# Whole-row spectrum stores, a later lambda product and bias loads on another queue in a two-block transformer kernel

## The chip, the cores and the metric

The kernel runs on one core of a Trainium2 chip. The core has a matrix engine (PE, with a separate track PEld for loading weights), a vector engine (DVE), an activation engine (ACT), a general engine (POOL) and a synchronising engine (SP). SP, ACT and POOL also issue DMA transfers; the trace calls these queues SPq, ACTq and POOLq. Each engine runs its own instructions strictly in order. The metric is device time in microseconds for one execution, and lower is better.

## The reference, cut to what matters

Two transformer blocks run over 512 tokens of 1024 features. The first has four mixers (a differential attention, a neighbourhood attention, a pooling and a long convolution), then a mixture of experts; the second has windowed attention and a state-space branch. The change touches the first block's opening: the filters of the long convolution, the modulation vectors, and one scalar of the differential attention.

```python
def hyena_filters(L, w1, b1, w2, b2, w3, b3):
    ...
    h = jnp.sin(HY_SIN_FREQ * (z @ w1.astype(F32) + b1.astype(F32)))
    h = jnp.sin(HY_SIN_FREQ * (h @ w2.astype(F32) + b2.astype(F32)))
    h = (h @ w3.astype(F32) + b3.astype(F32)).reshape(L, HY_ORDER, 2, HY_CH)
    ...
def bidir_long_conv(u, h_fwd, h_bwd, d_skip):
    k = jnp.concatenate([h_fwd, jnp.zeros_like(h_fwd[:1]), h_bwd[:0:-1]], axis=0)
    y = jnp.fft.irfft(jnp.fft.rfft(uf, n=2 * L, axis=1) * jnp.fft.rfft(k, axis=0)[None], ...)[:, :L]
...
mod_l = jnp.split(jax.nn.silu(c) @ lp['ada_w'] + lp['ada_b'], 6, axis=-1)
lam = jnp.exp(jnp.sum(lv[0] * lv[1])) - jnp.exp(jnp.sum(lv[2] * lv[3])) + lam_init
```

The filters go through two small layers with a sine, and a third layer. Their spectrum (real and imaginary part, for two convolutions) is wanted later, when the convolution multiplies in the frequency domain. `mod_l` scales and shifts the normed tokens, so that no projection can start before it.

## The kernel before, in words

The stage concerned is the opening, roughly the first 100 of 1294 us. The order of each engine's instructions is written by a planner that follows the program's order as a priority and fills in later instructions when it believes an engine free; so an instruction can run ahead of lines that stand above it (DVE runs L851 to L852 before L471). `tc.issue_after(x)` puts the instructions of its block behind `x` on x's engine.

- **Loads.** SP issues the small filter weights, the decay table, four blocks of x (L441), two of ctx (L444), eight blocks of `ada_w` of 1 MB each (L448), then the later weights. ACT issues `vec`, `ident`, `misc`, `rowsb` (L243, a row broadcast to 128 partitions) and the four loads of the modulation bias into `ab0` (L454). POOL issues the Fourier tables.
- **Filter layers** (L465 to L480): for each layer PE multiplies, ACT adds the bias (L469), five DVE instructions reduce the angle (L471 to L475), and ACT takes the sine. The DVE folding of the third layer's weights (L487) is held behind the last of these by `hold`.
- **Lambda product** (L851, recorded at the helper's line L252): DVE multiplies two parts of `rowsb`, and L852 sums them; the exponential comes much later (L854).
- **Third layer and filters** (L493 to L502), then `fold_filter` (a fold by DVE, a cast by ACT and a remainder by DVE, through the helper `split`, L254 to L256), for part 1 (sine) and part 0 (cosine) of convolutions o = 0 and 1.
- **Spectra** (`spectrum`, L574): for each part, o and half f2, PE forms two blocks of 128 frequencies by 256 channels, ACT copies them into a tile `ko` (two buffers, L581), and an ACT-issued DMA stores `ko` into the DRAM buffer `kspec` (256 KB). For part 0, f2 = 0, an extra row, the top frequency, is stored at frequency row 0 in the columns of part 1 (L588). Before the change the part 1, f2 = 0 store leaves that row out, with two DMAs: partitions 1 to 127, and row 0's second block.
- **Modulation**: PE multiplies the eight `ada_w` blocks between the spectra (L346); DVE adds the bias `ab0` (in `ada_end`, recorded at L249, tile `ab`); PE transposes (L363), and `norm_k` transposes and scales the tokens (L528 to L535). Then the projections begin.

Of the kernel before, what the change touches and what calls it, by code (L numbers as in the profile page):

```python
# [224 lines left out]
def tile_model(ctx: ExitStack, tc: tile.TileContext, A, out):  # L225
    nc = tc.nc
    V, SC, G, SY, TE = nc.vector, nc.scalar, nc.gpsimd, nc.sync, nc.tensor
# [23 lines left out]
    def mul(o, a, b, eng=None):  # L251
        (eng or V).tensor_tensor(o, a, b, op=ALU.mult)  # L252
# [79 lines left out]
    def nm(s="t"):  # L332
        bn[0] += 1
        return f"{s}{bn[0]}"
# [50 lines left out]
    def dft_mm(ps, tbl, part, fc, vh, vl, dfx, mid=None):  # L385
        fs = slice(fc * P, fc * P + P)
        sg = int(part != (fc >= 2))
        x = (None, (0, 1), (1, 0), (1, 0))[fc] if part == 0 else (None, None, (2, 1), (2, 1))[fc]
        for tt in (1, 0):
            mm3(ps, tbl[:, 0, tt, fs], tbl[:, 1, tt, fs], vh[:, sg, tt], vl[:, sg, tt], tt == 1,  # L390
                tt == 0 and x is None)
            if tt == 1 and mid is not None:
                mid()
        if x is not None:
            c = dfx[0:1, x[0] * P:x[0] * P + P]
            TE.matmul(ps, c, vh[0:1, x[1], 0], start=False, stop=False)
            TE.matmul(ps, c, vl[0:1, x[1], 0], start=False, stop=True)

    def nyq_mm(ps, altc, vh, vl, alone):
        for n, (tt, v) in enumerate(((0, vh), (0, vl), (1, vh), (1, vl))):  # L400
            TE.matmul(ps, altc, v[:, 0, tt], start=alone and n == 0, stop=alone and n == 3)
# [8 lines left out]
    with tc.tile_pool(name="pz", bufs=8, space=PSUM, reuse_waits="tile") as pz, \  # L410
            tc.tile_pool(name="fl", bufs=1, side="right", reuse_waits="tile") as fl, \
            tc.tile_pool(name="nrm", bufs=1, reuse_waits="tile") as nrm:
        def bank0():
            return pz.tile([P, 512], F32, tag="b", name=nm("pz"))
# [36 lines left out]
        ab0 = fl.tile([P, S], F32, name="ab0")  # L451
        G.memset(ab0, 0.0)
        for j in range(4):
            SC.dma_start(ab0[32 * j:32 * j + 2], A["ada_b"][0:1, 512 * j:512 * j + 512]  # L454
                         .partition_broadcast(2).rearrange("p o f -> p (o f)"))
        dfx = fl.tile([1, 384], F32R, name="dfx")
        G.dma_start(dfx, A["dfx"][:, 0:384])
# [7 lines left out]
        for layer, w in ((0, fw1), (1, fw2)):  # L465
# [9 lines left out]
            hold = V.tensor_scalar(f, f, PI_SAFE, -PI_SAFE, op0=ALU.min, op1=ALU.max)  # L475
# [8 lines left out]
        with tc.issue_after(hold.ins):  # L484
            for n, op in ((0, ALU.add), (1, ALU.subtract)):
                f3 = fw3.rearrange("p (o d c) -> p o d c", o=2, d=2)
                V.tensor_tensor(w3[:, :, n], f3[:, :, 0], f3[:, :, 1], op=op)  # L487
        fw3 = w3.rearrange("p o d c -> p (o d c)")


        filt = fl.tile([P, 4, 2, 2, 256], F32, name="filt")
# [82 lines left out]
        def spectrum(n, part, o, f2):  # L574
            ph, pl = phs[n]
            c0 = o * 512 + part * 256
            ko = fl.tile([P, 2, 256], F32, tag="ko", name=nm("ko"), bufs=2)
            for j in range(2):
                ps = bank0()[:, :256]
                dft_mm(ps, tbls[part], part, 2 * f2 + j, ph, pl, dfx)  # L580
                SC.copy(ko[:, j], ps)  # L581
            dst = kspec[2 * f2:2 * f2 + 2, :, c0:c0 + 256].rearrange("f p c -> p f c")
            if f2 == 0 and part == 0:
                V.tensor_scalar_mul(ko[0:1, 0], ko[0:1, 0], 0.5)
                ps = bank0()[0:2, :256]
                nyq_mm(ps, altc, ph, pl, True)
                V.tensor_scalar_mul(row0[:, o], ps[0:1], 0.5)
                SC.dma_start(kspec[0, 0:1, c0 + 256:c0 + 512], row0[:, o])  # L588
            if f2 == 0 and part == 1:
                SC.dma_start(dst[1:], ko[1:])  # L590
                SC.dma_start(dst[0:1, 1], ko[0:1, 1])
            else:
                SC.dma_start(dst, ko)

        steps = ((1, 0), (1, 1), (0, 0), (0, 1))
        aps = bank0()
# [2 lines left out]
        for f2 in range(2):  # L599
            spectrum(0, *steps[0], f2)  # L600
            ada_mm(f2, aps, araw[f2])
        filt_norms()
        for f2 in range(2):
            spectrum(1, *steps[1], f2)
            ada_mm(2 + f2, aps, araw[2 + f2])
# [11 lines left out]
        for k in range(4):  # L617
            spectrum(2 + k // 2, *steps[2 + k // 2], k % 2)
            norm_k(2 + k)
# [228 lines left out]
    lam = root.tile([P, 4], F32, name="lam")  # L848
    lp = root.tile([P, 2, 32], F32, name="lp")
    lv = rowsb[:, 16:144].rearrange("p (a b d) -> p a b d", a=2, b=2)  # L850
    mul(lp, lv[:, :, 0], lv[:, :, 1])  # L851
    V.tensor_reduce(lam[:, 0:2], lp, axis=AX.X, op=ALU.add)  # L852
    with tc.issue_after(hold_l.ins):
        SC.activation(lam[:, 0:2], lam[:, 0:2], AF.Exp)  # L854
# [1436 lines left out]
```

## Time and profile before

| what | us |
|---|---|
| median of 3 runs | 1297.05 |
| lowest and highest run | 1296.15, 1300.52 |
| the profiled execution, its own time | 1295.71 |
| its span in the profile | 1293.8 |

The profiled execution's time is 1.91 us more than its span, which lies around the profiled instructions. The granted PE clock was 0.946 of full speed over the span. Times in the trace count from the start of the span.

### The profile page before, as it was taken

The numbers are of one execution on the slowest core, as the hardware profiler recorded it, in microseconds if no ns is written. First come the engines' busy times: TensorE is split into PE (matmuls) and PEld (weight loads), VectorE is DVE, ScalarE is ACT, GpSimd is POOL, SyncE is SP. The second block draws the span as 40 slices with busy tenths as digits, with TensorE's granted clock in tenths as the row PEclk, the third lists the DMA queues.
The fourth block names the chain that finished last, engine by engine and source line by source line (L and its number), as shares of the span: only waits on it lengthen the run. The fifth ranks groups of instructions, "written<-read, shape, count | busy, mean of one in ns | idle before, by whom it ended". The sixth has DMA issues, their size and how long they took to land. (4 is left out here: it accounts for less than half of the span.)

```text
span 1293.8 us, 16003 instructions
## 1 busy us (share of the span) xinstructions
PE 1118.5 (86%) x5904; PEld 807.1 (62%) x5904; DVE 837.2 (65%) x1498; ACT 514.7 (40%) x907; POOL 210.4 (16%) x204
## 2 busy tenths in 40 slices
PE   3859979998588893999998999589799888899997
PEld 1447966675367772557464675368567676777785
DVE  3654365655678667428475897566954987977754
ACT  4252244443364232315243462344457332443532
POOL 1223500001610023100000000041400343130100
PEclk9978989999699996999999999899899999889999
DMA  9532714536612383988989995455121222223421
GB/s 345 199 106 81 174 62 135 195 131 193 180 50 98 99 272 117 314 305 325 367 305 384 334 353 205 156 196 173 50 65 46 82 78 82 78 78 119 153 70 65
DMA packets 132721, 220.61 MB, mean 171 GB/s; under 512 B 23645, under 2 KB 64793, under 8 KB 128795
## 3 DMA queue, kind: packets, MB, share of 16 engines
q1 hardware_dynamic: 122789, 196.04, 44.2%
q0 software_dynamic: 7104, 21.00, 5.5%
q10 hardware_dynamic: 2742, 2.46, 0.6%
q8 instruction: 49, 0.80, 0.3%
q14 instruction: 37, 0.30, 0.1%
HBM read 205.26 MB, written 11.04 MB: 167 GB/s over the span
## 5 line engine op out<-in xcount | busy, mean ns | idle before, releaser
L246 DVE TENSOR_TENSOR wl<-raw,wh 128x1024 fp32r<-128x1024 f32 x94 | 117.7, 1258 | 92.0 <-ACT wh L255 86.6
L255 ACT CAST wh<-raw 128x1024 fp32r<-128x1024 f32 x94 | 97.1, 1047 | 141.3 <-PE pf L260 66.0
L259 PE MATMUL pf<-r,wh 128*128 128x512 f32 x304 | 127.3, 421 | 8.1 <-DVE sg L252 3.0
L260 PE MATMUL pf<-r,wh 128*128 128x512 f32 x304 | 125.6, 414 | 0.7 <-DVE r L246 0.6
L261 PE MATMUL pf<-r,wl 128*128 128x512 f32 x304 | 125.4, 413 | 0.0
L249 DVE TENSOR_TENSOR r<-r,pb 128x512 f32<-128x512 f32 x88 | 55.0, 681 | 38.0 <-PE pb L1594 37.9
L259 PEld LDWEIGHTS pf<-r,wh 128*128 128x128 f32 x304 | 60.1, 198 | 24.9 <-DVE sg L252 3.5
L259 PE MATMUL pb<-wh,gh 128*128 128x512 f32 x176 | 70.5, 401 | 1.4 <-ACT wh L255 1.3
L260 PE MATMUL pb<-wl,gh 128*128 128x512 f32 x176 | 70.0, 398 | 0.8 <-DVE wl L246 0.7
L261 PE MATMUL pb<-wh,gl 128*128 128x512 f32 x176 | 69.9, 397 | 0.1
L260 PEld LDWEIGHTS pf<-r,wh 128*128 128x128 f32 x304 | 60.5, 199 | 15.1 <-DVE r L246 1.7
L261 PEld LDWEIGHTS pf<-r,wl 128*128 128x128 f32 x304 | 60.0, 197 | 14.7 <-issue 1.3
L246 DVE TENSOR_TENSOR wl<-r,wh 128x1024 fp32r<-128x1024 f32 x36 | 42.8, 1218 | 12.2 <-ACT wh L255 12.0
L255 ACT CAST wh<-r 128x1024 fp32r<-128x1024 f32 x36 | 37.1, 1054 | 22.4 <-DMA r<-in_moe_w_dram 12.8
L259 PE MATMUL ps<-r,wh 128*128 128x512 f32 (+1 forms) x112 | 44.0, 393 | 1.6 <-ACT at L867 1.5
L867 ACT COPY at<-ps 128x512 f32<-128x512 f32 x64 | 28.4, 481 | 40.4 <-PE ps L866 40.2
L261 PE MATMUL ps<-r,wl 128*128 128x512 f32 (+1 forms) x112 | 42.7, 381 | 0.0
L260 PE MATMUL ps<-r,wh 128*128 128x512 f32 (+1 forms) x112 | 42.6, 381 | 0.0
L259 PEld LDWEIGHTS pb<-wh,gh 128*128 128x128 f32 x176 | 33.2, 189 | 10.4 <-ACT wh L255 1.9
L1244 PE MATMUL pb<-xr,gw 128*64 128x512 f32 x136 | 39.6, 627 | 0.0
L1244 PE MATMUL pb<-r,gw 128*64 128x512 f32 x136 | 38.1, 598 | 1.3 <-DMA r<-in_moe_w_dram 1.3
L260 PEld LDWEIGHTS pb<-wl,gh 128*128 128x128 f32 x176 | 33.2, 189 | 9.3 <-DVE wl L246 1.9
(687 smaller groups left out, 2833.4 us busy)
## 6 DMA issues: line engine op xcount, KB each, us to landing
r<-in_moe_w_dram SPq DMA_DIRECT2D x42, 1024.0 KB
xr<-in_moe_w_dram SPq DMA_DIRECT2D x36, 1024.0 KB
raw<-in_w_in_dram SPq DMA_DIRECT2D x27, 1024.0 KB
r<-in_ada_w_dram SPq DMA_DIRECT2D x22, 1024.0 KB
raw<-in_moe_w_dram SPq DMA_DIRECT2D x18, 1024.0 KB
raw<-in_w_out_dram SPq DMA_DIRECT2D x8, 1024.0 KB
tb<-in_dft_dram POOLq DMA_DIRECT2D x4, 1024.0 KB, 7.1
itb<-in_idft_dram POOLq DMA_DIRECT2D x2, 1032.0 KB, 9.0
```

The source lines that it names most:

```text
L246: (eng or V).tensor_tensor(o, a, b, op=ALU.subtract)
L249: return (eng or V).tensor_tensor(o, a, b, op=ALU.add)
L255: SC.copy(hi, src)
L259: TE.matmul(ps, lh, rh, start=start, stop=False)
L260: TE.matmul(ps, lh, rl, start=False, stop=False)
L261: TE.matmul(ps, ll, rh, start=False, stop=stop)
L867: SC.copy(at[:, a:a + n].rearrange("p k q -> p (k q)"), pt[:, :n * P])
L1244: TE.matmul(ps[c], lh[:, k, c], raw[:, k * 512:k * 512 + 512], start=first and k == 0, stop=last and k == 3)
```

## The change

Three edits. The bias loads into `ab0` are issued by SP instead of ACT. The lambda product is held behind the last DVE instruction of the second filter layer. The part 1, f2 = 0 spectra are stored as whole tiles in one DMA each, so that row 0 of part 1 is first stored with that tile's row and later written over by the top-frequency row.

```diff
         for j in range(4):
-            SC.dma_start(ab0[32 * j:32 * j + 2], A["ada_b"][0:1, 512 * j:512 * j + 512]
+            SY.dma_start(ab0[32 * j:32 * j + 2], A["ada_b"][0:1, 512 * j:512 * j + 512]
                          .partition_broadcast(2).rearrange("p o f -> p (o f)"))
...
         fw3 = w3.rearrange("p o d c -> p (o d c)")
+        hold_f = hold
...
                 SC.dma_start(kspec[0, 0:1, c0 + 256:c0 + 512], row0[:, o])
-            if f2 == 0 and part == 1:
-                SC.dma_start(dst[1:], ko[1:])
-                SC.dma_start(dst[0:1, 1], ko[0:1, 1])
-            else:
-                SC.dma_start(dst, ko)
+            SC.dma_start(dst, ko)
...
     lv = rowsb[:, 16:144].rearrange("p (a b d) -> p a b d", a=2, b=2)
-    mul(lp, lv[:, :, 0], lv[:, :, 1])
+    with tc.issue_after(hold_f.ins):
+        mul(lp, lv[:, :, 0], lv[:, :, 1])
     V.tensor_reduce(lam[:, 0:2], lp, axis=AX.X, op=ALU.add)
```

## Rows read from the trace of the kernel before

**Rows 1.** The page: the span, and PE's busy time, share and instructions

```profile
span 1293.8 us, 16003 instructions
PE 1118.5 (86%) x5904; PEld 807.1 (62%) x5904; DVE 837.2 (65%) x1498; ACT 514.7 (40%) x907; POOL 210.4 (16%) x204
```

**Rows 2.** Stretches: length, busy per engine (instructions), granted PE clock, DMA share, GB/s

```profile
21.98:37.40 15.42, 13.99 (x17) 5.70 (x18) 8.23 (x14) 12.64 (x22) 4.88 (x4) 1.00 1.01 424
37.40:49.00 11.60, 11.60 (x69) 5.62 (x69) 10.13 (x17) 2.55 (x5) 6.36 (x3) 1.00 0.91 325
49.00:51.10 2.10, 2.10 (x15) 1.70 (x15) 2.10 (x9) 1.51 (x4) 0.00 (x0) 1.00 0.01 4
51.10:58.70 7.60, 7.60 (x59) 5.07 (x62) 2.31 (x9) 0.03 (x1) 0.00 (x0) 1.00 0.06 19
120.00:160.00 40.00, 40.00 (x275) 35.86 (x274) 17.41 (x25) 9.14 (x14) 18.93 (x39) 1.00 0.64 151
600.00:800.00 200.00, 193.13 (x859) 121.89 (x858) 145.63 (x187) 83.63 (x105) 3.95 (x4) 1.00 0.86 317
```

**Rows 3.** Timeline of PE after 56 us (start, length, work, [idle before and releaser])

```profile
56.54 2.78 PE L346 MATMUL pz<-r,sc 128*32 128x512 f32 x24
75.49 1.08 PE L363 MATMUL pz<-ident,ab 128*128 128x128 f32 x4 [16.17 <-ACT ph L255]
76.37 1.06 PE L528 MATMUL pz<-ident,xs 128*128 128x128 f32 x4
...
88.12 0.60 PE L528 MATMUL pz<-ident,xs 128*128 128x128 f32 x4
```

**Rows 4.** Timeline of DVE around the modulation bias

```profile
74.10 0.69 DVE L246 TENSOR_TENSOR ph<-fold,ph 128x512 fp32r<-128x512 f32 x1 [12.42 <-ACT ph L255]
74.71 0.68 DVE L249 TENSOR_TENSOR ab<-ab,pz 128x512 f32<-128x512 f32 x1
```

**Rows 5.** Timeline of ACT and its queue, 50 to 75 us

```profile
51.05 7.64 ACTq L591 DMA_DIRECT2D kspec<-ko  x1
58.73 0.37 ACT L581 COPY ko<-pz 128x256 f32<-128x256 f32 x1 [7.60 <-issue]
...
59.15 0.40 ACTq L593 DMA_DIRECT2D kspec<-ko  x1
59.59 0.61 ACT L255 CAST ph<-fold 128x512 fp32r<-128x512 f32 x1
64.23 0.65 ACT L581 COPY ko<-pz 128x256 f32<-128x256 f32 x2 [4.03 <-DMA kspec<-ko]
...
65.18 7.62 ACTq L591 DMA_DIRECT2D kspec<-ko  x1
72.90 0.65 ACT L581 COPY ko<-pz 128x256 f32<-128x256 f32 x2 [8.03 <-issue]
```

**Rows 6.** Timeline of DVE in the filter layers

```profile
12.72 0.23 DVE L252 TENSOR_TENSOR lp<-rowsb 128x64 f32<-128x64 f32 x1 [9.48 <-DMA rowsb<-in_rows_dram]
...
13.11 0.41 DVE L471 TENSOR_SCALAR sk<-sf 64x512 f32<-64x512 f32 x1
...
25.48 0.69 DVE L252 TENSOR_TENSOR filt<-pz,decay 128x512 f32<-128x512 f32 x1 [2.23 <-PE pz L496]
```

**Rows 7.** Timeline of ACT and its queue in the filter layers

```profile
7.38 0.68 ACT L469 ACTIVATE sf<-pz,fb 64x512 f32<-64x512 f32 x1 [2.65 <-DMA fb<-in_hy_b_dram]
8.09 3.70 ACTq L454 DMA_DIRECT2D ab<-in_ada_b_dram  x4
15.90 0.63 ACT L478 ACTIVATE h1e<-sf 64x512 f32<-64x512 f32 x1 [7.83 <-DVE sf L475]
```

**Rows 8.** Timeline of SP's queue

```profile
4.94 10.28 SPq L441 DMA_DIRECT2D xs<-in_x_dram  x4
...
32.78 0.33 SPq L234 DMA_DIRECT2D bones<-in_bones_dram  x1
```

**Rows 9.** Line L588, the top-frequency row's stores: ns, first and last start

```profile
L588 ACTq DMA_DIRECT2D kspec<-row x2: 244/260/275, 85.2 to 88.8; - x2
```

## The prediction

> **What bounds the kernel now.** I read the page first. PE is busy 86% of the 1293.8 us [rows 1], so what can be won is where PE stands still, or where its clock is low. I then listed PE's longest waits and cut the opening into stretches. The reader should compare the stretches [rows 2] with PE's timeline [rows 3]: from 120 to 160 us PE is busy all of the time, but before that it finishes the last `ada_w` products at 56.54 + 2.78 = 59.32 us and then does nothing for 16.17 us, until the transposes of the modulation (L363) at 75.49. This is PE's longest single wait in the kernel.
>
> The trace names ACT's cast of `ph` as what ended that wait. The bias add that L363 needs is a DVE instruction at 74.71, and directly ahead of it on DVE stands a remainder that waited 12.42 us for the cast [rows 4]. ACT's cast was late because ACT was held: the timeline of ACT and its queue [rows 5] shows two issues of the single-row DMA L591 that take 7.64 and 7.62 us, where L593, the store of a whole tile, takes 0.40. Between them ACT waits 4.03 us more for a `ko` buffer, which the first of these stores had not let go: the buffer came free at 64.23, 13.2 us after 51.05. So in this stage a store sets the end, although the DMA engines are nearly idle: their mean busy share from 51.1 to 58.7 us is 0.06, about one engine in 16, at 19 GB/s [rows 2].
>
> The second place is at the start. ACT has the first filter layer's angles ready at 7.38 + 0.68 = 8.06, but DVE takes them up only at 13.11, because the lambda product stands ahead of them and waits until 12.72 for `rowsb` [rows 6, 7].
>
> **Edit 1: whole-tile stores.** Removed: for each o, the DMA of partitions 1 to 127 and the single-row DMA behind it. Added: one whole-tile DMA each, priced at the 0.40 us of L593 [rows 5]; the same destination in the other columns and the same source tile, so this is the nearest row. By the rows the first partial store held its buffer 13.2 us. The Trainium skill ("DMA: Bandwidth & Descriptors", section "Why a DMA increments its semaphore by 16 and not by 1") says that a copy of 127 partitions runs on one DMA engine and one of 128 on sixteen; the share of 0.06 above agrees. By that page's 27 GiB/s for an engine the 254 KB would take an estimated 9.0 us, 4 less than the row, and the sum would lose nearly that much; it goes by the rows.
>
> What is late next? After the first pair of stores ACT has left, until the cast that frees the bias add: five `ko` copies at about 0.33 to 0.37, four casts at 0.61 and three stores at 0.40, together 1.8 + 2.4 + 1.2 = 5.4 us [rows 5]. From 51.1 on, that fits ahead of 59.3 even with some waits for PE, which ends its last spectrum at 56.54 [rows 3]; from there ACT needs two copies, one store and two casts, 0.7 + 0.4 + 1.2 = 2.3 us, to 58.9. DVE then needs one remainder (0.69) for the last-but-one cast, and the bias add (0.68) [rows 4], which can't start before PE's 59.32. So L363 starts at about 59.32 + 0.68 + 0.1 = 60.1 instead of 75.49: 15.4 us. If the whole-tile stores held the two buffers a few us longer than I think, some 3 us would be lost; the lower bound is 12, the upper 15.4, because PE itself is next.
>
> The top-frequency row now overwrites bytes of an earlier store, so ACT must wait for that store before L588. The Trainium skill's "DMA: Bandwidth & Descriptors", section "Two DMAs through the same engine are not ordered", speaks against the edit here: a DMA that touches what an earlier one writes has to wait for its completion, and by that page's fixed cost of about 2 us per DMA, two such waits at full length would be an estimated 4 us of held ACT. By the rows they cost nothing: L588 is issued at 85.2 and 88.8 us [rows 9], the stores that it must follow at 51.05 and 65.18 at the latest [rows 5], and even moved up by 15.4 us the first row store comes 18 us behind its tile's store. Queued behind it would be ACT's copies and `norm_k`. I take zero; the upper bound, from the 13.2 us that a buffer was held even by the slow store, is still zero.
>
> **Edit 2: lambda product behind the second layer.** DVE takes the angles up at 8.1 instead of 13.11: 5.0 us. The two small instructions go to a place where DVE waits anyway: ahead of the first filter product it idles 2.23 us, and they need 13.11 - 12.72 = 0.39 [rows 6]. Its reader, the exponential of L854, is held behind `norm_k` in the code. The shift reaches PE only if what follows is loaded 5 us earlier too. The sine comes at 10.9 instead of 15.90. The x blocks are issued between 4.94 and 15.22 [rows 8], and the DMA engines are saturated (1.01 at 424 GB/s) until 37.4 and 0.91 until 49 [rows 2]. The last PE products with `ada_w` would move from 56.54 to 51.5, and the load traffic ends by 49.0 (share 0.01 after that). So I take the whole 5.0, with a lower bound of 1 if the x blocks or the early `ada_w` blocks come too late.
>
> **Edit 3: bias loads on SP.** This takes 3.70 us from ACT's queue, 8.09 to 11.79 [rows 7]. Alone it is worth nothing, since ACT then waits 7.83 us for DVE. Beside edit 2 ACT is wanted for the sine at 10.9, so it keeps 0.9 of the 5.0 us. In exchange the four loads stand on SP behind the eight `ada_w` blocks. The next load there, `bones`, was issued at 32.78 [rows 8]; the bias loads would go out about then and land with the traffic ahead of them by 49. They are wanted at 59.3 - 5.0 = 54.3. Cost zero, with 5 us to spare.
>
> **Clock.** After the 16 us pause four transposes take 1.06 us at 76.37, and 0.60 at 88.12 [rows 3]. PE's first 4 us or so after the pause run slowly; without the pause the most that could come back is about half of it. ACT and DVE pace part of this stretch: I take 1.0, between 0 and 2.
>
> **Sum.** 15.4 + 5.0 + 1.0 = 21.4 us. What follows is a chain of PE work with loads whose start hangs on buffers released by PE and DVE, so the shift should be carried to the end. The profiled execution took 1295.71 us (span 1293.8 and 1.9 around it): 1295.7 - 21.4 = 1274.3. It stands 1.3 below the median of the runs, so for a median I say 1275.5.
>
> **The rivals.**
> - *The start is held by loads.* DMA engines are saturated until past 37 us [rows 2], so an earlier filter chain may only wait for x or `ada_w`. Against it: the end of PE's opening lies 7 us after the traffic. Then 4 to 5 us are lost: 1280. Chance 0.12.
> - *The lead is absorbed later.* From 600 to 800 us the DMA share is 0.86 at 317 GB/s [rows 2]; if weight loads set the pace there, half of the lead could be lost: 1286. Against it: PE is busy 193 of 200 us there. Chance 0.12.
> - *More than the sum.* The planner writes a new order for the opening, with PE's later 2 to 6 us waits shorter: about 1266. Chance 0.07.
> - *The stores stay slow.* If the 7.6 us came from the destination's rows and not from the 127 partitions, only the start is won, and perhaps not all of it: 1292 to 1294. L593's 0.40 us to the same buffer speaks against it [rows 5]. Chance 0.03; counted as no change.
> - *Slower: the biases come late.* The bias add holds DVE and with it L363. Each us that the four loads land after 54.3 costs one; from 54.3 + 21.4 = 75.7 on the kernel is slower than before. That the queue is first drained at 49 speaks against it; if the loads were held on SP until the 78 us or so, the time is 1300. Chance 0.04.
>
> **Numbers.** My forecast has the remaining 0.62 and a range of its own of 1271 to 1280 (the lower bounds of edit 1 and 2 don't fall together). With the two rivals above it and the one below taken in as far as they reach, 1266 to 1286 leaves out less than 2 in 10. Faster by over 0.3% (3.9 us, about what can be told from no change): 0.62 + 0.12 + 0.12 + 0.07 = 0.93; within it 0.03; slower 0.04.
>
> **What the profile after would show.** Right: no ACTq issue of some 7.6 us; PE's wait before L363 at 1 us or less and L363 at 54 to 56 us; L471 first at 8.1; L487 five us earlier; a DMA share well above 0.06 while `kspec` is stored; the first projection (L259 into `psw`) at some 77 to 79 us instead of 99.05. Wrong: a wait of DVE for the tile `ab` on a DMA; ACT waiting for x blocks after the second sine; L588 waiting for `kspec`; a lead at 100 us that is smaller at 1000.

## The result, and the profile after

The changed kernel took 1276.12 us (median, 1275.22 to 1277.83) against 1296.6 us for the kernel before in the same comparison. The ratio is 0.9848 with a 95% interval of 0.9816 to 0.9879: faster by 20.5 us, where 1275.5 was forecast. The profiled execution took 1276.5 us with a span of 1274.2, 19.6 us less than before.

The page's first lines show that no work went away, only standing time; they answer to [rows 1].

```profile
span 1274.2 us, 16002 instructions
PE 1120.6 (88%) x5904; PEld 808.4 (63%) x5904; DVE 837.6 (66%) x1498; ACT 514.8 (40%) x907; POOL 210.2 (17%) x204
```

PE's timeline, which answers to [rows 3], shows the pause before the modulation's transposes (L363) reduced from 16.17 us to 0.91. L363 starts at 60.05 instead of 75.49, 15.4 us earlier, and the first projection (`psw`) at 80.72 instead of 99.05, 18.3 us earlier. The four transposes right behind L363 take 0.60 instead of 1.06.

```profile
55.49 3.64 PE L346 MATMUL pz<-r,sc 128*32 128x512 f32 x32
60.05 0.63 PE L363 MATMUL pz<-ident,ab 128*128 128x128 f32 x4 [0.91 <-issue]
60.51 0.60 PE L529 MATMUL pz<-ident,xs 128*128 128x128 f32 x4
...
80.72 0.50 PE L259 MATMUL psw<-r,wh 128*128 128x512 f32 x1 [4.73 <-DVE hf L534]
```

ACT's queue, which answers to [rows 5]: the store of part 1, f2 = 0 (first and third line) is now issued in about 0.4 us like the others, and there is no issue of 7.6 us. The top-frequency row (L589) is issued without a wait.

```profile
46.42 0.39 ACTq L590 DMA_DIRECT2D kspec<-ko  x1
48.26 0.38 ACTq L590 DMA_DIRECT2D kspec<-ko  x1
52.92 0.37 ACTq L590 DMA_DIRECT2D kspec<-ko  x1
56.01 0.37 ACTq L590 DMA_DIRECT2D kspec<-ko  x1
65.28 0.37 ACTq L590 DMA_DIRECT2D kspec<-ko  x1
65.86 0.48 ACTq L589 DMA_DIRECT2D kspec<-row  x1
```

DVE's timeline, against [rows 6] and [rows 4]: the angles are taken up at 8.21 instead of 13.11, the lambda product runs in the gap ahead of the first filter, and the bias add waits for PE's products, not for the biases.

```profile
8.21 0.42 DVE L471 TENSOR_SCALAR sk<-sf 64x512 f32<-64x512 f32 x1 [4.88 <-ACT sf L469]
...
18.66 0.21 DVE L252 TENSOR_TENSOR lp<-rowsb 128x64 f32<-128x64 f32 x1
...
59.26 0.69 DVE L249 TENSOR_TENSOR ab<-ab,pz 128x512 f32<-128x512 f32 x1 [1.44 <-PE pz L346]
```

What is new is in the stretches (columns as in [rows 2]). From 43.4 to 51 us PE's granted clock is 0.51, the lower of its two levels (1.2 instead of 2.4 GHz); a closer cut of the same trace has 0.50 from 44 to 53 us, with PE busy 9.00 of these 9 us. Before, the same spectra ran at 1.00. They now last from 43.19 to 55.49, 12.3 us; before, they lasted from 48.84 to 56.54, 7.7 us. So a start that was 5.6 us earlier became an end that was 1.1 earlier.

```profile
38.00:43.40 5.40, 4.50 (x37) 2.46 (x34) 4.68 (x10) 1.29 (x3) 2.71 (x1) 1.00 0.45 188
43.40:51.00 7.60, 7.60 (x31) 5.58 (x30) 4.67 (x17) 2.53 (x6) 0.00 (x0) 0.51 0.22 74
51.00:55.50 4.50, 4.50 (x24) 3.87 (x23) 1.97 (x5) 1.64 (x4) 0.00 (x0) 0.69 0.67 220
```

The same spectra before:

```profile
48.84:56.54 7.70, 7.70 (x56) 6.25 (x53) 4.57 (x17) 1.54 (x4) 0.00 (x0) 1.00 0.04 13
```

Even that 1.1 is used up by the products behind the spectra: 32 of them stand there now and 24 before [rows 3], since the planner moved one `ada_w` block. PE ends them at 55.49 + 3.64 = 59.13, before at 59.32.

SP's queue shows the bias loads (L454) spread over 14.8 us, and the next weights (L313) issued from 51.37 on; before, they were issued from 40.60 on.

```profile
34.32 14.80 SPq L454 DMA_DIRECT2D ab<-in_ada_b_dram  x4
...
51.37 6.58 SPq L313 DMA_DIRECT2D raw<-in_w_in_dram  x2
```

SP's waits name what held the bias loads: a spectrum store on another queue (9.3 us more fell to loads of `ada_w`).

```profile
SPq L454 <- DMA kspec<-ko: 11.6, 1, 11.6
```

Why a load into `ab0` should wait for a store out of `ko` the trace does not tell.

### The profile page after: what moved, and what is told of

It reads as the page before. It is cut to its first block, busy times and chain, and to the rows that moved or that the text cites. A ratio compares the mean times of both kernels' runs of the same rounds, so it can differ in the third digit from the quotient of the medians.

```text
span 1274.2 us, 16002 instructions
## 1 busy us (share of the span) xinstructions
PE 1120.6 (88%) x5904; PEld 808.4 (63%) x5904; DVE 837.6 (66%) x1498; ACT 514.8 (40%) x907; POOL 210.2 (17%) x204
```

## The experiments

Two theories stood against each other. By the first, the stores are the whole gain and the 5 us of the earlier filter layers were lost to the clock on the way. By the second, which is the forecast's sum, both parts count. All runs in one table; the ratio is to the kernel before, run beside each (its medians there lie between 1294.64 and 1296.6). "L363" and "first projection" are PE's starts in the profiled execution; in e4, e5 and e8 the same transposes are recorded at L364.

| kernel | median us | ratio, 95% interval | L363 | first projection | span |
|---|---|---|---|---|---|
| before | 1296.6 | | 75.49 | 99.05 | 1293.8 |
| changed | 1276.12 | 0.9848 (0.9816 to 0.9879) | 60.05 | 80.72 | 1274.2 |
| e1, stores alone | 1275.95 | 0.9855 (0.9826 to 0.9884) | 59.30 | 81.53 | 1274.1 |
| e2, all but the stores | 1294.41 | 0.9987 (0.9967 to 1.0006) | 70.97 | 95.41 | 1291.7 |
| e3, split 120 and 7 | 1275.35 | 0.9847 (0.9822 to 0.9871) | 59.92 | 82.54 | 1271.3 |
| e9, split 122 and 5 | 1286.03 (one run) | | 59.67 | 89.47 | 1283.9 |
| e5, all products early | 1275.35 | 0.9835 (0.9800 to 0.9870) | 55.26 | 77.39 | 1272.1 |
| e4, fifth product early | 1274.87 | 0.9853 (0.9820 to 0.9886) | 55.17 | 77.39 | 1270.7 |
| e7, bias loads on ACT | 1273.57 | 0.9836 (0.9808 to 0.9865) | 55.56 | 77.78 | 1268.5 |
| e8, e4 and edge clearing | 1271.78 | 0.9827 (0.9796 to 0.9857) | 55.92 | 75.00 | 1268.8 |
| e10, e7 and edge clearing | 1272.03 | 0.9816 (0.9789 to 0.9843) | 54.87 | 73.95 | 1270.1 |

A span is not read closer than some 3 us: e3 has its first projection 1.8 us later than the changed kernel and still a span 2.9 us shorter.

**e1, the stores alone.** The kernel before with one edit:

```diff
-            if f2 == 0 and part == 1:
-                SC.dma_start(dst[1:], ko[1:])
-                SC.dma_start(dst[0:1, 1], ko[0:1, 1])
-            else:
-                SC.dma_start(dst, ko)
+            SC.dma_start(dst, ko)
```

> The kernel before with the whole-tile stores alone; lambda product and bias loads stay where they were. Theory (the stores are the whole gain, since the early lead of the changed kernel was lost to a lower PE clock before L363): no ACT queue issue of 7.6 us, PE clock 1.00 from 43 to 59 us, last ada_w products end near 59.3, L363 at about 60, time within 2 us of the changed kernel's 1276. Rival (the earlier filter layers are worth their 5 us): 1281 or more.

For the time, the first theory holds: the stores alone give what the three edits give. That the clock took the rest is not shown by e1; e4 and e7 bear on it. PE's stretch and its timeline in e1: full clock through the spectra, and L363 at 59.30, even a little ahead of the changed kernel, with DVE's angles about as late as before (12.90).

```profile
48.40:55.50 7.10, 7.10 (x51) 5.75 (x49) 5.95 (x20) 4.17 (x10) 0.00 (x0) 1.00 0.42 113
```

```profile
55.60 2.78 PE L346 MATMUL pz<-r,sc 128*32 128x512 f32 x24
59.30 0.63 PE L363 MATMUL pz<-ident,ab 128*128 128x128 f32 x4 [0.91 <-issue]
```

**e2, all but the stores.** The changed kernel with the five removed lines of e1 put back.

> The changed kernel with the partial stores of the kernel before put back; lambda product and bias loads stay changed. Theory: L471 starts at 8.2, the two 7.6 us issues are back and set L363, which comes some 4 to 5 us earlier than in the kernel before (about 71), because ACT and not PE sets the pace there: 1291 to 1293. Rival (a lead at the start is always lost before L363): 1296 to 1297.

The mechanism is as expected and the time isn't clear: the 7.4 us issue is back, and L363 comes 4.5 us earlier than before. Of these 4.5 us 3.6 are left at the first projection and 2.1 in the span; the medians differ by 1.2, 1294.41 lies between the range expected and the rival's, and the interval reaches over 1. e2 doesn't measure edit 2 alone either: the bias loads on SP went out only at 58.55, the next weights at 73.08, and ACT waited 2.79 us for those weights ahead of its cast at 78.44. Lines of ACT's queue and of PE:

```profile
45.81 7.40 ACTq L592 DMA_DIRECT2D kspec<-ko  x1
```

```profile
70.97 1.09 PE L363 MATMUL pz<-ident,ab 128*128 128x128 f32 x4 [16.34 <-DVE ab L249]
```

**e3 and e9, other partial stores.** The changed kernel with row 0 left out again, cut at 8 (e3) or at 6 (e9):

```diff
-            SC.dma_start(dst, ko)
+            if f2 == 0 and part == 1:
+                SC.dma_start(dst[8:], ko[8:])
+                SC.dma_start(dst[1:8], ko[1:8])
+                SC.dma_start(dst[0:1, 1], ko[0:1, 1])
+            else:
+                SC.dma_start(dst, ko)
```

> The changed kernel, but row 0 is left out of the part 1, f2 = 0 stores as before, with other shapes: partitions 8 to 127 (120 of them), 1 to 7, and row 0's second block, three DMAs each. Theory (127 partitions in one DMA are what held ACT): each issue takes 0.2 to 0.5 us, L363 at 60 to 62, time 1276 to 1279. Rival (any store that leaves row 0 out, or the single-row DMA, is slow): an issue of several us stays and the time is 1284 to 1292.

> The changed kernel with row 0 left out of the part 1, f2 = 0 stores again, as partitions 6 to 127 (122 = 2 x 61 of them), 1 to 5, and row 0's second block. Theory (a copy runs on the largest divisor up to 16 of its partition count: 1 engine for 127, 2 for 122, 15 for 120): ACT is held about half as long as the 7.6 us, 3 to 4.5 us per store, with a DMA share near 0.13 meanwhile, and the time is 1277 to 1285. Rival (127 is a special case and any even count is fast): issues below 1 us, 1276.

In e3 ACT issues the first three DMAs in 0.60, 0.29 and 0.27 us, and the time is that of the changed kernel (1275.35, just under the 1276 to 1279 expected). So neither leaving row 0 out nor the single-row DMA was slow; the copy of 127 partitions was.

```profile
46.35 0.60 ACTq L591 DMA_DIRECT2D kspec<-ko  x1
46.99 0.29 ACTq L592 DMA_DIRECT2D kspec<-ko  x1
47.32 0.27 ACTq L593 DMA_DIRECT2D kspec<-ko  x1
```

In e9 the copy of 122 partitions runs at a DMA share of 0.13 and 44 GB/s, where the one of 127 ran at 0.06 and 19 GB/s [rows 2]: about two engines against one. The rule of the Trainium skill that the prediction cited ("DMA: Bandwidth & Descriptors", section "Why a DMA increments its semaphore by 16 and not by 1") puts 127 partitions on one engine, and these runs agree with it. But ACT was not held 3 to 4.5 us; the issues behind the two copies took 0.69 and 0.96 us, so that part of the expectation fell. The time, 1286.03 in the one run there is, went another way. SP waited 22.2 us with a bias load for the first of these stores, issued the next weights at 63.30, and ACT waited 6.29 us for them in the middle of the token scaling. That the bias loads do wait for this store is borne out by four runs: the last of them goes out at 48.9 in the changed kernel and 49.9 in e3, where the store is fast, at 55.3 in e9, and at 59.4 in e2, where the copy of 127 partitions is back. ACT's queue and stretches of e9, then SP's waits, then waits of all engines:

```profile
46.76 0.69 ACTq L592 DMA_DIRECT2D kspec<-ko  x1
...
55.56 0.96 ACTq L592 DMA_DIRECT2D kspec<-ko  x1
```

```profile
52.30:54.30 2.00, 2.00 (x12) 1.73 (x12) 0.49 (x1) 0.00 (x0) 0.00 (x0) 0.79 0.13 44
```

```profile
SPq L454 <- DMA kspec<-ko: 22.2, 1, 22.2
```

```profile
ACT wh L255 <- DMA raw<-in_w_in_dram: 6.3, 1, 6.3
```

**e5 and e4, more work for PE ahead of the spectra.** The changed kernel with PE's order held by hand: all eight `ada_w` blocks (e5) or the first five (e4) ahead of the second half of the first spectra.

```diff
+        late = []
+        def ada_first():
+            for kc in range(5):
+                m = ada_mm(kc, aps, araw[kc])
+            late.append(m)
         for f2 in range(2):
             spectrum(0, *steps[0], f2)
-            ada_mm(f2, aps, araw[f2])
         filt_norms()
         for f2 in range(2):
-            spectrum(1, *steps[1], f2)
-            ada_mm(2 + f2, aps, araw[2 + f2])
-        for kc in range(4, KC):
+            with tc.issue_after(late[-1].ins):
+                spectrum(1, *steps[1], f2)
+        for kc in range(5, KC):
             ada_mm(kc, aps, araw[kc])
```

The diff is that of e4; in e5 both fives are eights. `ada_first` is called inside the first spectrum between its two halves; the second halves, and the small transposes, are held behind `late` in the same way.

> The changed kernel with PE's order at the opening written by hand: all eight ada_w blocks are multiplied ahead of the second half of the first spectra, where PE waits for the filters between 38 and 43 us; then the first spectra, the small transposes and the second spectra. Theory (PE's clock fell at 43 us because PE had little to do before it): clock 1.00 through the spectra, these take some 8 us instead of 12.3, and 3.6 us of products no longer stand behind them: L363 at 52 to 54 and 1268 to 1271. Rival 1 (the clock falls all the same): L363 at about 56.5, 1272 to 1274. Rival 2 (the bias loads, the last of which SP issues at 48.9, are next): DVE waits for a DMA of the tile ab, and less than 4 us are won.

> The changed kernel with PE's order held so that the fifth ada_w block (8 matmuls, which the planner put behind the spectra in the changed kernel) is multiplied ahead of the second half of the first spectra, as in the kernel before. Theory (PE had waits and light work from 38 to 43 us, and its clock fell for the spectra behind them): with 0.9 us more work there the clock stays at 1.00 from 43 to 54, the spectra take about 8 us and L363 starts at 55 to 56 instead of 60.05; the time is 1271 to 1274, as far as the later stages keep it. Rival (the clock falls there whatever the order): 0.50 after 43 us, L363 near 59, 1275 to 1277.

In e5 the clock fell earlier instead: 0.84 and 0.81 are the means of the two stretches, after PE had stood waiting (3.88 us busy of 5.40); from 47.7 on it was at 1.00. L363 came at 55.26, later than the 52 to 54 expected, and the time, 1275.35, missed the 1268 to 1271.

```profile
38.00:43.40 5.40, 3.88 (x28) 1.57 (x25) 4.68 (x9) 1.29 (x3) 2.38 (x1) 0.84 1.04 375
43.40:47.70 4.30, 4.30 (x33) 1.11 (x26) 3.00 (x14) 0.62 (x1) 0.00 (x0) 0.81 0.98 278
```

In e4 the clock stayed at 1.00 from 38 to 51 us, and L363 came at 55.17, 4.9 us earlier than in the changed kernel, as expected. At the first projection 3.3 of these are left, because PE waits 6.29 us for DVE there instead of 4.73. The time, 1274.87, lies above the 1271 to 1274 expected and is not told apart from the changed kernel's by the intervals.

```profile
38.00:43.40 5.40, 4.71 (x42) 2.42 (x40) 4.68 (x10) 1.29 (x3) 2.59 (x1) 1.00 0.46 186
43.40:51.00 7.60, 7.58 (x54) 6.04 (x50) 6.19 (x21) 4.07 (x10) 0.00 (x0) 1.00 0.31 98
```

**e7, the bias loads back on ACT.** The changed kernel without edit 3:

```diff
-            SY.dma_start(ab0[32 * j:32 * j + 2], A["ada_b"][0:1, 512 * j:512 * j + 512]
+            SC.dma_start(ab0[32 * j:32 * j + 2], A["ada_b"][0:1, 512 * j:512 * j + 512]
```

> The changed kernel with the four bias loads back on ACT's queue (edits 1 and 2 alone). Theory (edit 3 is worth at most the 0.9 us of the prediction, and moved an ada_w block in PE's order): the sine of layer 1 starts at about 11.8 instead of 11.0, the next weights (L313) are issued near 40 instead of 51.4, the fifth block is back ahead of the spectra, PE's clock stays up and L363 starts at 56 to 57; 1272 to 1275. Rival (the bias loads on SP were needed for the early start): layer 1's sine at 13 or later and L363 at 60 or later, 1276 to 1279.

The first layer's sine started at 11.17 instead of 11.01: edit 3 is worth at most 0.16 us there, not 0.9 (with edit 3 in place it started at 11.13 in e2 and 11.31 in e3). Without it the planner writes the fifth block ahead of the spectra again, PE's clock stays at 1.00, the next weights are issued from 35.87 on, and L363 starts at 55.56. The time, 1273.57, is in the range expected, but its interval overlaps the changed kernel's. A line of ACT and one of PE's stretches in e7:

```profile
11.17 0.63 ACT L478 ACTIVATE h1e<-sf 64x512 f32<-64x512 f32 x1 [2.96 <-DVE sf L475]
```

```profile
43.40:51.00 7.60, 7.60 (x54) 5.65 (x49) 6.51 (x21) 3.69 (x10) 0.00 (x0) 1.00 0.79 256
```

**e8 and e10, what is late next.** In the changed kernel PE still waits 4.73 us for DVE ahead of the first projection (6.29 in e4 and e7). POOL clears two whole tiles there, ahead of its last token scalings. e8 is e4, and e10 is e7, with only those columns cleared that are never written (64 of 1088 and 12 of 3084):

```diff
-    G.memset(pool_u, 0.0)
-    G.memset(hyu, 0.0)
+    for a_, b_ in ((0, 16), (528, 544)):
+        G.memset(pool_u[:, :, a_:b_], 0.0)
+    for a_ in (0, 513):
+        G.memset(hyu[:, :, a_:a_ + 1], 0.0)
```

> The kernel of e4, and POOL clears only the edge columns of hyu and pool_u that are never written (34 columns of 1088 and 12 of 3084 or so) instead of the whole tiles. Theory (after the stores, what is late next in the opening is the tail of the token scaling, where POOL's two memsets of 1.0 and 2.95 us stand ahead of its last three scalings, DVE waits for their buffers, and PE waits 4.7 us for DVE): the wait of the first projection falls to 1 to 3 us, another 2 to 4 us are won against e4: 1268 to 1271. Rival (ACT's chain of scalings sets this tail): less than 1 us against e4.

> The kernel of e7 (whole-tile stores, later lambda product, bias loads on ACT) with the edge-only memsets of e8. Theory (the two gains stand in different places of the opening and add): L363 near 55.5, the first projection at about 75, time 1269 to 1271.5, the fastest so far. Rival (the 2 to 3 us at the first projection are given back later): no different from e7, 1273 to 1275.

POOL's timeline in the changed kernel, and then in e8:

```profile
75.84 1.01 POOL L624 MEMSET pool_u<- 128x1088 f32 x1 [1.11 <-PE pz L529]
76.78 2.95 POOL L625 MEMSET hyu<- 128x3084 f32 x1
79.71 4.98 POOL L536 TENSOR_SCALAR r<-hf,AB1c 128x256 fp32r<-128x256 f32 x3
```

```profile
71.70 0.19 POOL L638 MEMSET pool_u<- 128x32 f32 x2 [1.12 <-PE pz L533]
```

The expectation looked for a wait of DVE for POOL's buffers, but DVE waited only 0.17 us for POOL in the changed kernel and not at all in e4. What is late are DVE's own scalings. While POOL clears, one that takes 0.5 us elsewhere takes 1.03 and 1.52 in the changed kernel and 3.63 in e4 and e7, and it ends about 0.3 us after the clearing (77.13 after 76.85, 80.01 after 79.73). In e8 and e10 it takes 0.49. So the two are shown to go together; why DVE is slow beside the clearing is not. DVE's timeline in the changed kernel, and then in e8:

```profile
76.10 1.03 DVE L536 TENSOR_SCALAR r<-hf,AB 128x512 fp32r<-128x512 f32 x1
...
78.49 1.52 DVE L536 TENSOR_SCALAR r<-hf,AB 128x512 fp32r<-128x512 f32 x1
```

```profile
71.96 0.49 DVE L540 TENSOR_SCALAR r<-hf,AB 128x512 fp32r<-128x512 f32 x1
```

PE's wait for DVE fell from 6.29 to 3.15 us in both. e8's first projection came at 75.00, 2.4 us ahead of e4's; e10's came at 73.95, 3.8 us ahead of e7's. By the medians these are the fastest kernels here: 1271.78 and 1272.03. Both miss their expected ranges a little, and e10's 3.8 us are no longer seen in its median, which is 1.5 below e7's. Their intervals still overlap the changed kernel's.

e8 also shows that e4's order of products does not keep the clock up by itself: with the same order it fell to 0.81 and 0.84 over two stretches, and L363 came 0.75 us later than in e4.

```profile
38.00:43.40 5.40, 3.94 (x32) 1.55 (x24) 4.68 (x10) 1.29 (x3) 1.98 (x1) 0.81 0.47 192
43.40:47.70 4.30, 4.30 (x29) 2.77 (x22) 2.60 (x13) 2.13 (x6) 0.00 (x0) 0.84 0.18 61
```

## Why the prediction was right, step by step

**Edit 1** was sized right: 15.4 us expected at L363, and e1, which has this edit alone, brings it 16.19 us earlier (75.49 to 59.30) and gives the whole gain. That the changed kernel shows 15.44 there, with edit 2 in it as well, is no second proof. PE was next, as forecast, and the bias add waited for its last products. That the 127 partitions made the store slow, and not the destination, is shown by e3; e9 shows the bandwidth doubling with the second engine, though the hold on ACT all but goes. The row that is written over later cost nothing, as the rows had it; the wait that the Trainium skill asks for ("DMA: Bandwidth & Descriptors", section "Two DMAs through the same engine are not ordered") found a store that was long done: L589 comes 19 us behind its tile's store (65.86 and 46.42) and was issued in 0.48 us.

**Edit 2** was right in its mechanism, and its 5.0 us were lost by L363. DVE started 4.9 us earlier, PE's third layer 4.5 us, and the spectra 5.6 us. The step that failed is "I take the whole 5.0": I looked for loads that could hold the start, and those came in time. What was late next was, in the trace, not a load but the clock of PE itself: 12.3 us for spectra that took 7.7, with the moved block behind them. My lower bound of 1 us was the truer figure, for another reason. L363 was forecast at 54 to 56 us and came at 60.05, and the first projection at 77 to 79 and came at 80.72; e4 and e7 put L363 at 55.2 and 55.6, with the clock up. That these 4 to 5 us reach the time is not shown: the medians of e4 and e7 are 1.3 and 2.6 us below the changed kernel's, and e7, which is edits 1 and 2, is 2.4 below e1, which is edit 1; all of these intervals overlap.

**Edit 3** was taken at zero with 0.9 us inside edit 2. In e7 it is at most 0.16. It had two effects that the prediction lacked. I said that the four loads would go out at about 32.8; the first did at 34.3, but the last only at 48.9, behind a store of ACT's. And the planner, given the new queue, moved a block of PE's products behind the spectra. Neither cost time by itself that the medians show, but e9 shows how close it was: with a slower store ahead of them, the same queue brought the weights too late, and 10 us went in its one run.

**Clock after the pause**: 1.0 us taken, between 0 and 2. From L363 to the first projection 20.67 us passed instead of 23.56, so 2.9 us came back. The same 120 products take 18.04 us before, at a mean clock of 0.88, and 15.94 now, at 1.00: 2.1 us are the clock, a little over my upper bound, and the other 0.8 a shorter wait for DVE (4.73 instead of 5.52). PE's stretches, before and then after (length, busy, clock, DMA share, GB/s):

```profile
75.49:93.53 18.04, 18.04 (x120) 0.88 0.35 118
```

```profile
60.05:75.99 15.94, 15.94 (x120) 1.00 0.35 108
```

**The sum** of 21.4 us thus met 20.5 (19.6 in the span) with its second term missing and its third too small: 15.4, then 2.9 at the first projection, and 1.3 more over the rest of the kernel, which is within what one profile can tell. That the time came out 0.6 us from the forecast is in part luck: of the 5.0 us that were lost, 3.2 were made up by what the sum had too small or did not have. The lead of 18.3 us at the first projection was carried to the end, so the rival of a lead absorbed later, and the one of loads at the start, both fell. So did late biases: 1.44 us of waiting, for PE.

**Open.** Why the clock fell in the changed kernel is not settled. Ahead of the fall PE had waits and light products (4.50 us busy of 5.40 from 38.0 to 43.4), and e3 and e9, with the same order of PE's products, fell to 0.50 at the same place. But e2, with that order too, had 4.61 and kept 1.00 (its stretches below). With one more block there it stayed up in e4, and yet not in e8. Each kernel has one trace, so it isn't known either whether its other executions fall at that place. What else could decide was not tried.

```profile
38.00:43.40 5.40, 4.61 (x39) 2.70 (x36) 4.68 (x10) 1.29 (x3) 2.47 (x1) 1.00 0.42 173
43.40:51.00 7.60, 7.53 (x53) 5.87 (x52) 4.52 (x17) 1.50 (x4) 0.00 (x0) 1.00 0.05 15
```

## What to carry to other kernels

A long DMA issue on an engine that also computes is read as a wait of everything behind it: look at the partition count of that copy and of the one ahead of it before looking at its size. A start that comes earlier is only worth what survives the next stage, and PE's clock level belongs in that list as much as loads and buffers do. A DMA moved to another queue can meet waits there that it did not have before, everything behind it in that queue waits with it, and the order that the planner writes elsewhere can change too.

## What the runs showed of the hardware that was not expected

A 127-partition store of 254 KB held the issuing engine for 7.4 to 8.0 us at its next DMA (before and e2), while one of 122 partitions and 244 KB, on about twice the DMA bandwidth (44 against 19 GB/s), held it for 0.69 and 0.96 us (e9). So the hold is not in proportion to the transfer time; what lies between was not measured.

PE's clock went to the lower level and stayed there for at least 9 us although PE was busy throughout (9.00 of 9.00 us from 44 to 53 in the changed kernel, at 0.50), after a stretch with short waits only.

A DVE scaling that takes 0.5 us took up to 3.63 us while POOL cleared a tile, and 0.49 without that (e4 and e8).
